# Hybrid RWKV-7 and neighbourhood-attention block: two affine forms of a tanh moved from VectorE to ScalarE, and the filler matmuls laid anew

## Chip, cores and metric

The kernel runs on one core of a Trainium2 chip. The metric is the device time of one execution in microseconds (us). A time is given as the median of several runs.

## What is computed

One trunk layer on 512 tokens of width 2048: a norm, one combined projection, two branches that read it (RWKV-7 time mixing in two directions, and 2-D neighbourhood attention), an output projection, a gated per-layer embedding and a final norm. Cut to what matters here:

```python
z = rms_norm(h, norm_mix_g) @ w_in
zs = centred_shift_mix(z[..., :SHIFT_W], mu_prev, mu_next)
# RWKV branch, 16 heads of 64, two directions
decay = exp(-DECAY_SCALE * sigmoid(w0 + tanh(wd) @ w2))
iclr = sigmoid(a0 + ad @ a2)
kk = (k * k_k) normalised per head
k_dir = k * (1.0 + (iclr - 1.0) * k_a)
# per token: S = S diag(w) + (S a) b^T + v k^T;  y = S r,  with a = -kk, b = kk * iclr
y = scan(forward) + scan(reverse);  group norm, bonus, SiLU gate
# attention branch: clamped 8 x 16 windows, softmax, SiLU gate
h = h + concat(y_a, y_b) @ w_out
h = h + (p @ w_ple_proj) * sigmoid(rms_norm(h) @ w_ple_gate)
return rms_norm(h)
```

## The kernel before

Every large product is made in three passes on TensorE (PE): a weight tile of 128x512 is copied on ScalarE (ACT) to a rounded half `wh` (L140), VectorE (DVE) makes the rest `wl` (L141), and `one_step` issues for each 128-row block three matmuls of 512 columns (L159, L161, L163). There are three raw buffers and six of `wh` and of `wl`.

The RWKV part runs in **eight rounds**, one for each pair of heads `ct`. In round `ct` the scan of pair `ct` (`chain`, eight steps of three parts: `cw` L592, `cu` L609, `cs` L619) goes on beside the preparation of pair `ct + 1` (`prepare`, `stage`, `normal`, `solve`). Each part of a scan step ends in a short DVE copy or sum that the next part's matmuls read: `wt` L596, `uv` L613, `uv` L625. A prologue prepares pair 0 with no scan beside it. After the rounds come eight pairs of attention heads (`natten`), the output projection and the gated embedding.

In `prepare` each of the two directions `d` makes, from the small products `lw` and `la`: two tanh on ACT (L418 into `t1`, L420 into `t3`), `1 + tanh` (L421) and a running sum (L424) on DVE, two exponentials on ACT (L425, L426), then on DVE the two affine forms of `t3` (L428 into `t4`, which takes a buffer named `tq`; L429 in place), a small copy of chunk ends (L431), and products (L434 to L445) that the `L458` matmuls read.

TensorE's order is written out by hand: `ORDER` lists the steps of a round (`c4b` is part b of scan step 4, `p`/`s` are parts of `prepare`, `v`/`m` of `stage`, `f` of `finish`, `n` of `normal`, `q`/`z` of `solve`), and the number behind a name says how many of the large projections' matmuls ("fillers") are issued ahead of that step. `EDGE_FILL` gives other numbers for single rounds (-1 is the prologue, 100 to 107 the attention). Fillers come from one stream of projections that later steps need; what has not been issued by then is issued at once.

The order on ACT, DVE, GpSimd (POOL) and the load queue is a scheduler's. `W_AHEAD` and `HOP` rank instructions ahead of what was written before them: `W_AHEAD` the weight loads, `wh` and `wl`; `HOP` the short DVE instructions of the scan. Every engine then works its own list strictly in order.

Of the kernel before, what the change touches and what calls it, by code (L numbers as in the profile page):

```python
# [10 lines left out]
AF = mybir.ActivationFunctionType  # L11
ALU = mybir.AluOpType
# [8 lines left out]
LAM = math.exp(-0.5)  # L21
EPS = 1e-6
LNX_EPS = 64e-5
W_AHEAD = 1275
FIRST = (24, 25, 8)
SUM_AT = (6, 35)
AT2 = (40, 24)
# [1 line left out]
KEEP_AT = 3  # L29
P_AHEAD = 200  # L30
ORDER = (
# [3 lines left out]
)  # L35
NAT_ORDER = (
    "np t0:11 t1:19 S0:16 S2:16 S1:3 T0:16 S3:25 T2:15 A0:26 T1:8 T3:24 A1:11"
)
FILL = {t.partition(":")[0]: int(t.partition(":")[2] or 0) for t in (ORDER + " " + NAT_ORDER).split()}
ORDER, NAT_ORDER = ([t.partition(":")[0] for t in o.split()] for o in (ORDER, NAT_ORDER))  # L40
EDGE_FILL = {
# [9 lines left out]
}  # L51
HOP = 118

VEC = {}
_o = 0
# [8 lines left out]
def block_kernel(ctx: ExitStack, tc: tile.TileContext, xT, pT, win, wout, wpg, wpp, vec, w2, rpb,  # L64
# [323 lines left out]
    def prepare(ct, k, r, kk, bon):  # L388
        w2r = sp.tile([128, 2, 2, 128], F32, name="w2r", tag="t3", bufs=1)
        S_.dma_start(w2r[0:64], w2[ct])  # L390
        S_.dma_start(w2r[64:128], w2[ct])
        w2s = sp.tile([128, 16, C], F32R, name="w2s", tag="ga", bufs=1).rearrange("p u i -> p (u i)")
        w2h = w2s[:, 0:512].rearrange("p (d i o) -> p d i o", d=2, i=2)
        w2l = w2s[:, 512:768].rearrange("p (i o) -> p i o", i=2)
        A.activation(w2h, w2r, AF.Copy)
        for d in range(2):
            rows = slice(64 * d, 64 * d + 64)
            G_.tensor_tensor(w2l[rows], w2r[rows, d], w2h[rows, d].bitcast(F32), ALU.subtract)

        kx = sp.tile([128, 2, NCH, 3, C], F32, name="kx", tag="kx", bufs=2)  # L400
        rx = kx[:, :, :, 1, :]
        pc = sp.tile([128, 2, NCH], F32, name="pc", tag="pc", bufs=2)
        m1s = []
        for d in range(2):
            yield
            rows = slice(64 * d, 64 * d + 64)
            lps = []
            for i in range(2):
                ps = aux()
                P.matmul(ps, w2h[:, d, i, :], lora[:, i, d, :], start=True, stop=False)  # L410
                P.matmul(ps, w2l[rows, i, :], lora[rows, i, d, :], start=False, stop=True)
                lps.append(ps)
            lw, la = lps
            t12 = sp.tile([128, 2, NCH, C + 1], F32, name="t12", tag="t12", bufs=1)
            t1, t2 = t12[:, 0], t12[:, 1]
            G_.memset(t1[:, :, 0:1], 0.0)
            wb = 26 + 8 * d + ct
            A.activation(t1[:, :, 1:], dirv(lw, d), AF.Tanh, scale=0.5, bias=vd[:, wb:wb + 1])  # L418
            t3 = b2("t3", 1)
            A.activation(chv(t3), dirv(la, d), AF.Tanh, scale=0.5, bias=vd[:, wb + 16:wb + 17])  # L420
            V.tensor_scalar(t1[:, :, 1:], t1[:, :, 1:], 1.0, None, ALU.add)  # L421
            t1f = t1.rearrange("p c i -> p (c i)")
            t2f = t2.rearrange("p c i -> p (c i)")
            V.tensor_tensor_scan(t2f, multf, t1f, 0.0, ALU.mult, ALU.add)  # L424
            A.activation(t1f, t2f, AF.Exp, scale=-0.5 * LAM)  # L425
            A.activation(t2[:, :, 1:], t2[:, :, 1:], AF.Exp, scale=0.5 * LAM)  # L426
            t4 = b2("tq", 2)
            V.tensor_scalar(t4, t3, vd[:, 58 + ct:59 + ct], vd[:, 66 + ct:67 + ct], ALU.mult, ALU.add)  # L428
            V.tensor_scalar(t3, t3, -0.5, -0.5, ALU.mult, ALU.add)  # L429
            ei = t2[:, :, 1:]  # L430
            V.tensor_copy(pc[:, d, :], t1[:, :, C])  # L431
            for h in range(2):
                hr = slice(64 * h, 64 * h + 64)
                (G_ if h else V).tensor_tensor(kx[hr, d, :, 2 * h, :], dirv(kk, d)[hr], t1[hr, :, 0:64], ALU.mult)  # L434
            V.tensor_tensor(chv(t4), chv(t4), ei, ALU.mult)
            V.tensor_tensor(chv(t3), chv(t3), ei, ALU.mult)
            V.tensor_tensor(rx[:, d, :, ::(-1 if d else 1)], dirv(r, d), t1[:, :, 1:], ALU.mult)
            m1 = sp.tile([128, NCH, 128], F32, name="m1", tag="m1", bufs=2)
            for h in range(2):
                hr = slice(64 * h, 64 * h + 64)  # L440
                bcol = slice(64 * h, 64 * h + 64)
                kcol = slice(64 - 64 * h, 128 - 64 * h)
                if d:
                    kcol = slice(127 - 64 * h, 63 if h == 0 else None, -1)
                V.tensor_tensor(m1[hr, :, bcol], chv(t3)[hr], dirv(kk, d)[hr], ALU.mult)  # L445
                G_.tensor_tensor(m1[hr, :, kcol], chv(t4)[hr], dirv(k, d)[hr], ALU.mult)  # L446
            m1s.append(m1)

        ga = sp.tile([128, 16, C], F32, name="ga", tag="ga", bufs=1)
        gr = sp.tile([128, 2, 2, NCH, C], F32, name="gr", tag="gr", bufs=2)  # L450
        for d in range(2):
            for c0 in range(0, NCH, 4):
                yield
                pair = [aux(), aux()]
                for c in range(4):
                    for h in range(2):
                        hr = slice(64 * h, 64 * h + 64)
                        P.matmul(pair[h][:, c * 128:(c + 1) * 128], m1s[d][hr, c0 + c, :],  # L458
                                 kx[hr, d, c0 + c, h:h + 2, :].rearrange("p s i -> p (s i)"), start=True, stop=True)
                cs = slice(c0, c0 + 4)  # L460
                for h in range(2):
                    hr = slice(64 * h, 64 * h + 64)
                    kr = slice(64 - 64 * h, 128 - 64 * h)
                    sv = pair[h].rearrange("p (c s i) -> p c s i", c=4, s=2)
                    V.tensor_tensor(ga[hr, d * NCH + c0:d * NCH + c0 + 4, :], sv[hr, :, h, :],
                                    mask[hr, None, 0:64].to_broadcast([64, 4, C]), ALU.mult)
                    V.tensor_tensor(gr[:, h, d, cs, :], sv[:, :, 1 - h, :],
                                    (mg1[h] if d else mask[:, 64:128])[:, None, :].to_broadcast([128, 4, C]), ALU.mult)
                    V.tensor_tensor(kx[kr, d, cs, 2 * h, :], sv[kr, :, h, :],  # L469
                                    (mk1 if d else mask[:, 0:64])[kr, None, :].to_broadcast([64, 4, C]), ALU.mult)  # L470
        td = sp.tile([128, 32, 32], F32, name="td", tag="td", bufs=1)
        V.transpose(out=td, in_=ga.rearrange("p u (ib i) -> p i ib u", ib=2))
        tmp = b2("t3", 1)

        def blocks(i0, ni, j0, nj, step=(32, 1)):
            return bass.AP(tensor=td.tensor, offset=td.offset + i0 * 32 + j0,
                           ap=[list(td.ap[0]), [16 * 33, 2], [step[0], ni], [step[1], nj]])

        for m in range(1, 15):
            ni = 15 - m  # L480
            tv = tmp[:, 0:2 * ni * m].rearrange("p (b i j) -> p b i j", b=2, j=m)
            V.tensor_tensor(tv, blocks(m + 1, ni, m, m, (32, 0)), blocks(m, ni, 0, m, (0, 1)), ALU.mult)  # L482
            V.tensor_tensor(blocks(m + 1, ni, 0, m), blocks(m + 1, ni, 0, m), tv, ALU.add)
        V.memset(td.rearrange("p i j -> p (i j)")[:, ::33], 1.0)
        return m1s, kx, rx, pc, bon, td, ga, gr
# [620 lines left out]
```

## Time and profile before

| | us |
|---|---|
| median of 3 runs | 1684.52 |
| lowest, highest | 1677.0, 1687.58 |
| the profiled execution: time, span | 1671.64, 1669.9 |

In the page's busy times PE stands at 1560.0 us (93% of the span), DVE at 1044.3 (63%), ACT at 685.2 (41%), POOL at 302.9 (18%). The granted TensorE clock is 0.957 on average. The profiled execution is one of its own and 12.9 us under the median, so terms are worked out on its time and then set against the median. Busy shares are means over stages: the rounds lie at 159.8 to about 882 us, the attention up to about 1291 us.

### The profile page before, as it was taken

Reading aid. Unit: us, or ns where it says so; the run is one execution under the profiler, and the core shown is the slowest. Engines: PE = TensorE matmul, PEld = TensorE weight load, DVE = VectorE, ACT = ScalarE, POOL = GpSimd, SP = SyncE. Lnnn points to the kernel's source line nnn. Section 1 sums busy time; section 2 is a strip of 40 time slices with the busy share of each in tenths; the row PEclk is TensorE's granted clock in tenths of the full one; section 3 lists DMA queues with packets and bytes.
Section 4 is the critical chain, followed back from the end, with each engine's and each line's share of the span. In section 5 each row is a group of like instructions: output and inputs, shape, how many; then the busy total and the mean of one; then the engine's idle time right before and its main releaser. Section 6 shows DMA issues by size and latency. Waiting matters only on the chain.

```text
span 1669.9 us, 30779 instructions
## 1 busy us (share of the span) xinstructions
PE 1560.0 (93%) x12392; PEld 1210.9 (73%) x12392; DVE 1044.3 (63%) x2071; ACT 685.2 (41%) x1231; POOL 302.9 (18%) x318
## 2 busy tenths in 40 slices
PE   7969898998989899898999999999999999999995
PEld 5757576766757576675767777777877888888885
DVE  8786886858688685878646444554456544454435
ACT  6624162442616244251426344443445333343331
POOL 2021414223141322314113011111110000100001
PEclk9979998999999898899999999999999999999998
DMA  6202020110202011020115332323222433532203
GB/s 210 94 29 67 21 83 27 62 48 26 84 20 83 27 58 52 21 82 27 59 40 173 100 95 89 88 76 95 81 78 80 136 122 118 165 119 89 88 32 101
DMA packets 74351, 131.32 MB, mean 79 GB/s; under 512 B 7904, under 2 KB 16352, under 8 KB 74208
## 3 DMA queue, kind: packets, MB, share of 16 engines
q1 hardware_dynamic: 74208, 129.36, 24.2%
q8 instruction: 97, 1.59, 0.4%
q14 instruction: 46, 0.38, 0.1%
HBM read 123.03 MB, written 6.29 MB: 77 GB/s over the span
## 4 chain that ended last, share of the span: by engine, by line
PE 74%; DVE 15%; issue 4%; ACT 4%; POOL 2%; DMA 1%; SPq 0%; DVEq 0%; ACTq 0%; POOLq 0%
PE mm L163 19%; PE mm L159 18%; PE mm L161 18%; DVE wl L141 2%; PE cs L619 2%; PE aux L458 1%; PE cw L592 1%; PE ns L792 1%; ACT wh L140 1%; DVE m L445 1%; POOL m L446 1%; PE no L818 1%; PE cu L609 1%; PE nt L808 1%; DVE t L482 1%
## 5 line engine op out<-in xcount | busy, mean ns | idle before, releaser
L141 DVE TENSOR_TENSOR wl<-wraw,wh 128x512 fp32r<-128x512 f32 x384 | 283.1, 738 | 305.5 <-ACT wh L140 255.2
L140 ACT ACTIVATE wh<-wraw 128x512 fp32r<-128x512 f32 x384 | 240.9, 628 | 506.3 <-PE mm L161 421.5
L159 PE MATMUL mm<-xh,wh 128*128 128x512 f32 x1024 | 420.7, 411 | 0.0
L163 PE MATMUL mm<-xh,wl 128*128 128x512 f32 x1024 | 419.9, 410 | 0.0
L161 PE MATMUL mm<-xl,wh 128*128 128x512 f32 x1024 | 418.4, 409 | 0.0
L159 PEld LDWEIGHTS mm<-xh,wh 128*128 128x128 f32 x1024 | 197.0, 192 | 42.6 <-issue 1.3
L163 PEld LDWEIGHTS mm<-xh,wl 128*128 128x128 f32 x1024 | 196.6, 192 | 42.8 <-issue 1.3
L161 PEld LDWEIGHTS mm<-xl,wh 128*128 128x128 f32 x1024 | 196.6, 192 | 42.7 <-issue 1.1
L159 PE MATMUL mm<-ch,wh 128*128 128x512 f32 x256 | 99.9, 390 | 0.0
L161 PE MATMUL mm<-cl,wh 128*128 128x512 f32 x256 | 99.9, 390 | 0.0
L163 PE MATMUL mm<-ch,wl 128*128 128x512 f32 x256 | 99.9, 390 | 0.0
L163 PE MATMUL mm<-hh,wl 128*128 128x512 f32 x224 | 87.3, 390 | 0.0
L161 PE MATMUL mm<-hl,wh 128*128 128x512 f32 x224 | 87.2, 389 | 0.0
L159 PE MATMUL mm<-hh,wh 128*128 128x512 f32 x224 | 87.1, 389 | 0.0
L604 POOL TENSOR_TENSOR stp<-uv,pc 64x128 f32<-64x128 f32 x96 | 56.1, 584 | 141.3 <-DVE uv L627 69.6
L768 POOL TENSOR_TENSOR bm<-text,nm 128x256 f32<-128x256 f32 x48 | 37.9, 818 | 237.5 <-DVE mx L794 193.0
L458 PE MATMUL aux<-kx,m 64*128 64x128 f32 x512 | 47.1, 306 | 14.7 <-DVE kx L469 7.5
L458 PEld LDWEIGHTS aux<-kx,m 64*128 64x128 f32 x512 | 38.6, 204 | 29.3 <-issue 20.1
L592 PE MATMUL cw<-uv,kx 128*64 128x64 f32 (+1 forms) x512 | 40.8, 248 | 18.9 <-DVE uv L625 17.7
L592 PEld LDWEIGHTS cw<-uv,kx 128*64 128x64 f32 (+1 forms) x512 | 28.4, 145 | 38.0 <-DVE uv L625 25.5
L163 PEld LDWEIGHTS mm<-ch,wl 128*128 128x128 f32 x256 | 48.1, 188 | 10.1
L159 PEld LDWEIGHTS mm<-ch,wh 128*128 128x128 f32 x256 | 48.1, 188 | 10.1 <-issue 0.2
(267 smaller groups left out, 2569.1 us busy)
## 6 DMA issues: line engine op xcount, KB each, us to landing
wraw<-in_win_dram SPq DMA_DIRECT2D x264, 256.0 KB
wraw<-in_wout_dram SPq DMA_DIRECT2D x64, 256.0 KB
wraw<-in_wpg_dram SPq DMA_DIRECT2D x56, 256.0 KB
xr<-in_xT_dram SPq DMA_DIRECT2D x32, 256.0 KB
out_dram<-h SPq DMA_DIRECT2D x16, 256.0 KB
text<-in_rpb_dram SPq DMA_DIRECT2D x16, 252.0 KB
w2r<-in_w_dram SPq DMA_DIRECT2D x16, 128.0 KB
cat<-bon SPq DMA_DIRECT2D x8, 256.0 KB
```

Of the source, the lines that this page charges most:

```text
L140: A.activation(wh, src, AF.Copy)
L141: V.tensor_tensor(wl, src, wh.bitcast(F32), ALU.subtract)
L159: P.matmul(ps, wh[:, sl], xh[kt], start=(kt == 0), stop=False)
L161: P.matmul(ps, wh[:, sl], xl[kt], start=False, stop=False)
L163: P.matmul(ps, wl[:, sl], xh[kt], start=False, stop=(kt == nk - 1))
L445: V.tensor_tensor(m1[hr, :, bcol], chv(t3)[hr], dirv(kk, d)[hr], ALU.mult)
L446: G_.tensor_tensor(m1[hr, :, kcol], chv(t4)[hr], dirv(k, d)[hr], ALU.mult)
L458: P.matmul(pair[h][:, c * 128:(c + 1) * 128], m1s[d][hr, c0 + c, :], kx[hr, d, c0 + c, h:h + 2, :].rearrange("p s i -> p (s i)"), start=Tr ...
L592: P.matmul(wps[hr, d * 64:(d + 1) * 64], kx[rows, d, c, 2 * h, :], uv[rows, c, h, d, :], start=True, stop=True)
L604: G_.tensor_tensor(sps[hr], uv[hr, c, h, :, :], pc[hr, :, c:c + 1].to_broadcast([64, 2, C]), ALU.mult)
L619: P.matmul(nps[hr, d * 64:(d + 1) * 64], mt[:, d, c, hr], uv[:, c, h, d, :], start=True, stop=True)
L768: G_.tensor_tensor(bm[:, kd].rearrange("p g r c -> p r g c"), text[:, ::-1, e1:(e1 - 32 if e1 > 31 else None):-1].rearrange("p r (g c) -> ...
```

## The change

The two DVE instructions L428 and L429 become ACT instructions in the same place of the program: an Identity with a scale and a bias per partition, and a Copy with two constants. `W_AHEAD` goes from 1275 to 4117 and `HOP` from 118 to 168. The numbers of fillers ahead of the steps are changed, most of them by one to five, and the attention's steps stand in another order. The changed file has three lines more, so its line numbers from the table on are higher by 3.

```diff
-W_AHEAD = 1275
+W_AHEAD = 4117
...
-    "pa p1:4 c0a c0b:2 c0c:2 c1a:2 c1b:1 c1c:4 p2:1 c2a c2b:4 c2c c3a:1 c3b:1 s0:2 c3c:3 c4a:1 c4b c4c "
+    "pa p1:4 c0a c0b:3 c0c:2 c1a:2 c1b:1 c1c:4 p2:1 c2a c2b:4 c2c c3a:1 c3b:1 s0:2 c3c:3 c4a:1 c4b c4c:1 "
...
-HOP = 118
+HOP = 168
...
-            V.tensor_scalar(t4, t3, vd[:, 58 + ct:59 + ct], vd[:, 66 + ct:67 + ct], ALU.mult, ALU.add)
-            V.tensor_scalar(t3, t3, -0.5, -0.5, ALU.mult, ALU.add)
+            A.activation(t4, t3, AF.Identity, scale=vd[:, 58 + ct:59 + ct], bias=vd[:, 66 + ct:67 + ct])
+            A.activation(t3, t3, AF.Copy, scale=-0.5, bias=-0.5)
```

The rest of the diff is the table: in a round `c7a` goes from 0 fillers to 3, `v1` from 1 to 4, `v2` from 6 to 7, `m0` from 14 to 9, `m2` from 4 to 1, `na` from 3 to 0. In the prologue `p2` goes from 7 to 2. In the last round's scan the fillers go from 64 to 74.

On DVE, round 3 (its fourth), from the `wt` copy of scan step 3 to that of step 4. Before (`t_4810` is t1 and t2 of direction 1, `t_4813` its t3):

```order
L596 COPY wt<-cw 128x128
L421 TENSOR_SCALAR t_4810<-t_4810 128x8x64
L424 SCALAR_TENSOR_TENSOR t_4810<-mult,t_4810 128x520
L613 COPY uv<-cu 64x128 x2
L428 TENSOR_SCALAR tq<-t_4813,vd 128x512
L431 COPY pc<-t_4810 128x8
L429 TENSOR_SCALAR t_4813<-t_4813 128x512
L434 TENSOR_TENSOR kx<-kk,t_4810 64x8x64
L141 TENSOR_TENSOR wl<-wraw,wh 128x512
L435 TENSOR_TENSOR tq<-tq,t_4810 128x512
L625 TENSOR_TENSOR uv<-cs,stp 64x128 x2
```

The same place in the changed kernel (lines higher by 3):

```order
L599 COPY wt<-cw 128x128
L424 TENSOR_SCALAR t_4811<-t_4811 128x8x64
L427 SCALAR_TENSOR_TENSOR t_4811<-mult,t_4811 128x520
L616 COPY uv<-cu 64x128 x2
L345 SCALAR_TENSOR_TENSOR zraw<-mm,rstdb 128x512
L144 TENSOR_TENSOR wl<-wraw,wh 128x512
L434 COPY pc<-t_4811 128x8
L437 TENSOR_TENSOR kx<-kk,t_4811 64x8x64
L438 TENSOR_TENSOR tq<-tq,t_4811 128x512
L628 TENSOR_TENSOR uv<-cs,stp 64x128 x2
```

The two affine forms are gone from between the two copies of the scan, and the evacuation of the gate's projection (L342 before, L345 now) has come in there from a place behind scan step 5.

On ACT, the same round, from its first tanh. Before:

```order
L418 ACTIVATE t_4704<-aux,vd 128x8x64
L420 ACTIVATE t_4707<-aux,vd 128x512
L425 ACTIVATE t_4704<-t_4704 128x520
L426 ACTIVATE t_4704<-t_4704 128x8x64
L140 ACTIVATE wh<-wraw 128x512
L418 ACTIVATE t_4810<-aux,vd 128x8x64
L420 ACTIVATE t_4813<-aux,vd 128x512
L140 ACTIVATE wh<-wraw 128x512
L425 ACTIVATE t_4810<-t_4810 128x520
L426 ACTIVATE t_4810<-t_4810 128x8x64
```

The same place in the changed kernel:

```order
L421 ACTIVATE t_4704<-aux,vd 128x8x64
L423 ACTIVATE t_4707<-aux,vd 128x512
L431 ACTIVATE tq<-t_4707,vd 128x512
L432 ACTIVATE t_4707<-t_4707 128x512
L428 ACTIVATE t_4704<-t_4704 128x520
L143 ACTIVATE wh<-wraw 128x512
L429 ACTIVATE t_4704<-t_4704 128x8x64
L421 ACTIVATE t_4811<-aux,vd 128x8x64
L423 ACTIVATE t_4814<-aux,vd 128x512
L431 ACTIVATE tq<-t_4814,vd 128x512
L143 ACTIVATE wh<-wraw 128x512
L428 ACTIVATE t_4811<-t_4811 128x520
```

The forms stand right behind the second tanh and ahead of the first exponential, in direction 0 both of them; a weight copy (L143 now) stands ahead of the second exponential of direction 0, where it stood behind it. No load of an activation table is added anywhere.

## Rows read from the trace of the kernel before

**Rows 1.** Windows by stage; stretch, length, PE, PEld, DVE, ACT, POOL, clock, DMA, GB/s.

```profile
0.00:159.80 159.80, 132.56 (x985) 103.07 (x985) 126.48 (x217) 83.04 (x137) 32.84 (x31) 0.91 0.32 103
159.80:837.60 677.80, 614.41 (x7309) 453.73 (x7308) 512.97 (x1056) 260.82 (x450) 183.02 (x198) 0.92 0.15 49
456.10:555.10 99.00, 90.72 (x1053) 66.92 (x1052) 75.25 (x153) 39.02 (x67) 26.64 (x29) 0.91 0.15 49
837.60:1640.00 802.40, 801.57 (x4018) 643.23 (x4016) 385.76 (x757) 335.48 (x634) 80.55 (x85) 1.00 0.31 97
```

**Rows 2.** Waits of PE; us in total, times, longest.

```profile
PE cs L619 <- DVE uv L613: 18.2, 22, 1.6
PE cw L592 <- DVE uv L625: 17.7, 10, 2.8
...
PE aux L458 <- DVE m L445: 6.1, 1, 6.1
```

**Rows 3.** Timeline of PE, round 3, scan steps 1 to 5; idle time in brackets.

```profile
461.45 0.45 PE L609 MATMUL cu<-wt,xt 64*64 64x64 f32 x8 [0.20 <-DVE wt L596]
...
478.77 0.77 PE L592 MATMUL cw<-uv,kx 128*64 128x64 f32 x8 [2.24 <-DVE uv L625]
...
480.67 0.69 PE L609 MATMUL cu<-wt,xt 64*64 64x64 f32 x8 [0.75 <-DVE wt L596]
482.59 1.07 PE L619 MATMUL cs<-uv,mt 128*64 128x64 f32 x7 [1.23 <-DVE uv L613]
...
488.38 0.40 PE L161 MATMUL mm<-xl,wh 128*128 128x512 f32 x1
488.62 0.39 PE L163 MATMUL mm<-xh,wl 128*128 128x512 f32 x1
```

**Rows 4.** Timeline of DVE, the same stretch.

```profile
474.66 0.55 DVE L428 TENSOR_SCALAR tq<-t,vd 128x512 f32<-128x512 f32 x1
475.13 1.14 DVE L431 COPY pc<-t 128x8 f32<-128x8 f32 x1
476.19 0.41 DVE L429 TENSOR_SCALAR t<-t 128x512 f32<-128x512 f32 x1
476.52 0.68 DVE L434 TENSOR_TENSOR kx<-kk,t 64x512 f32<-64x512 f32 x1
...
478.44 0.61 DVE L625 TENSOR_TENSOR uv<-cs,stp 64x128 f32<-64x128 f32 x2
...
489.32 0.67 DVE L342 SCALAR_TENSOR_TENSOR zraw<-mm,rstdb 128x512 f32<-128x512 f32 x1
```

**Rows 5.** Timelines of ACT and of POOL, the same stretch.

```profile
461.11 0.64 ACT L425 ACTIVATE t<-t 128x520 f32<-128x520 f32 x1 [4.15 <-DVE t L424]
...
473.55 0.63 ACT L140 ACTIVATE wh<-wraw 128x512 fp32r<-128x512 f32 x1 [1.00 <-PE mm L161]
474.16 0.64 ACT L425 ACTIVATE t<-t 128x520 f32<-128x520 f32 x1
...
474.88 1.37 POOL L434 TENSOR_TENSOR kx<-kk,t 64x512 f32<-64x512 f32 x1 [2.38 <-ACT t L425]
```

**Rows 6.** Groups by line and form; busy us, mean ns, idle before.

```profile
L428 DVE TENSOR_SCALAR tq<-t,vd 128x512 f32<-128x512 f32 x16 | 8.7, 544 | 0.2
L429 DVE TENSOR_SCALAR t<-t 128x512 f32<-128x512 f32 x16 | 8.0, 502 | 0.3
...
L426 ACT ACTIVATE t<-t 128x512 f32<-128x512 f32 x16 | 10.1, 631 | 0.5
...
L298 ACT ACTIVATE r<-zraw,vd 128x512 f32<-128x512 f32 x8 | 5.8, 725 | 6.1 <-DVE zraw L297 6.1
```

**Rows 7.** Windows of 3.4 us around scan step 4; columns as in rows 1.

```profile
476.80:480.20 3.40, 1.15 (x16) 0.81 (x16) 3.31 (x6) 0.00 (x0) 1.64 (x2) 1.00 0.23 77
480.20:483.60 3.40, 1.69 (x20) 1.32 (x22) 2.85 (x6) 0.00 (x0) 2.35 (x3) 0.50 0.00 0
483.60:487.00 3.40, 3.40 (x36) 2.65 (x32) 2.95 (x10) 0.00 (x0) 1.12 (x2) 0.50 0.00 0
```

**Rows 8.** Waits of ACT; us in total, times, longest.

```profile
ACT wh L140 <- PE mm L161: 453.2, 178, 15.3
```

More of the change, by code (lines that the diff above doesn't have):

```diff
@@ L31 @@
 ORDER = (
[3 rows of a table removed]
[3 rows of a table added]
 )
 NAT_ORDER = (
-    "np t0:11 t1:19 S0:16 S2:16 S1:3 T0:16 S3:25 T2:15 A0:26 T1:8 T3:24 A1:11"
+    "np:10 t0:21 t1:19 S0 S1:8 S2:22 T0:10 S3:20 T2:12 A0:14 T3:22 T1:12 A1:19"
 )
```

25 rows, old and new, of tables (EDGE_FILL, ORDER) are left out of this document.

## Prediction

> **What bounds the kernel now.** I read the windows by stage first [rows 1]. From 837.6 us to 1640 us, half of the span, PE is busy for 801.57 of 802.40 us at full clock: attention, output projection and gate are bound by TensorE, and since the change leaves every matmul in place, moving fillers there cannot win or lose much. The room is ahead of that. In the seven rounds with a preparation beside the scan (159.8 to 837.6 us) PE is idle for 677.80 - 614.41 = 63.4 us, about 9 us a round, and the clock is 0.92. In the prologue and the start it is idle for 159.80 - 132.56 = 27.2 us. Next come PE's waits [rows 2]: the largest name DVE's short scan instructions (uv after `cu`, uv after `cs`), and one of 6.1 us is the prologue's wait for the products of L445. So DVE's list is what PE waits for, though DVE is busy for only 75.25 of a round's 99.0 us: the waits gather where the preparation's long DVE instructions stand between the scan's short ones. In round 3 these are the waits ahead of step 4 and inside it, 2.24 + 0.75 + 1.23 = 4.2 us out of the round's 8.3 [rows 1, 3]. These repeat from round to round; over the whole kernel the first kind comes to 17.7 us [rows 2].
>
> **The change, part by part. What leaves DVE:** 16 times L428 and 16 times L429, 8.7 + 8.0 = 16.7 us or 2.1 us a round [rows 6]. That is the most a straight return could give in eight preparations. I follow one round to see how much of it PE gets.
>
> Direction 0: the forms stand at scan step 1. PE waits there for 0.20 us only [rows 3], since it is busy with its own list; the time that DVE wins up to step 2 is spent waiting for PE's next `cw`. The extra filler at `c0b` is paid there and saved where it came from. I take 0; the bounds are 0 and 1.0 us.
>
> Direction 1: here PE waits for the L625 that starts at 478.44. From the start of L428 at 474.66 to there DVE is busy without a break for 3.78 us [rows 4]. Start to start, L428 holds 475.13 - 474.66 = 0.47 and L429 0.33 us, so 0.8 us leave. But the gate's L342, 0.67 us, comes in at this very place. L431, a copy of 8 columns, takes 1.14 us here while POOL runs its own L434 from 474.88 for 1.37 us; it now stands later, so most of POOL's time lies beside L342 and the `wl` ahead of it, and I count 0.6 us less for it. Sum 0.8 - 0.7 + 0.6 = 0.7 us a round. If L431 keeps its length the sum is 0.1; if it shrinks to a few tenths and L342's place costs nothing, it is 1.6. I take 0.7, since POOL's instruction moves with the running sum and the overlap will not vanish whole.
>
> Then step 4: the new filler at `c4c` stands in the wait of 1.23 us, and takes work from a place where PE is never idle. A filler is worth 488.62 - 488.38 = 0.24 us at full clock and twice that at half [rows 3], so 0.35 us a round. L342 is gone from behind step 5 (489.32, rows 4); DVE waits for PE's L458 products more than the other way there, so I take 0.2 us, bounds 0 and 0.7. The three fillers at `c7a` and the fewer at `m0` and `m2` are moved between places where PE has next to no idle time: 0. A round gives 0.7 + 0.35 + 0.2 = 1.25 us, seven rounds 8.8 us.
>
> **What ACT takes on.** The Identity has two operands per partition. An ACT form with one takes 725 ns and one with none 631 ns [rows 6], so I estimate 0.82 us for two, and 0.63 us for the Copy. The pair costs 1.45 us, 23 us over 16 pairs. ACT is busy for 39 of 99 us in a round. In direction 0 it sits idle for 4.15 us ahead of L425, waiting for the running sum, and both forms fit in there [rows 5]. In direction 1 the Identity fits ahead of the weight copy that waits 1.00 us for PE, but the Copy stands between the two exponentials and delays L426 by 0.6 us; L435 reads that, and DVE reaches it only behind L434, later than L426's new end. So 0, and 0.3 us a round against if that cover is gone.
>
> **Prologue.** Here nothing but DVE is late. Each direction loses 0.54 + 0.50 us of forms, but the first exponential (0.64 us, rows 5) ran beside them and must now be waited for, so 0.4 us is left; in direction 0 the mix of `v` now fills that gap, and 1.1 us is left. Together 1.5 us, bounds 0 and 3.
>
> **The clock.** In the 3.4 us ahead of step 4 PE is busy for 1.15 us, and right behind it the granted clock falls to 0.50, that is from 2.4 to 1.2 GHz, and stays there for two such stretches, 6.8 us [rows 7]. With 0.7 us less idle time the fall may stay out in some rounds. The eight small matmuls of a `cu` take 0.45 us at full clock and 0.69 at half (461.45 and 480.67, rows 3), 0.24 us more, and about five such parts lie in the 6.8 us: 1.2 us a round. I take it in two to three of seven rounds, 3 us; bounds 0 and 8.4. It can also go the other way: a fall that comes earlier or lasts one window longer costs as much.
>
> **Attention and the rest.** PE has no idle time to win; a wait made anew by the other order of scores would show as idle PE. I take 0, and 4 us against.
>
> **Sum.** 8.8 + 1.5 + 3 = 13.3 us off the profiled execution's 1671.64, so 1658.3 us. The median of the runs is 12.9 us above that execution, and the forecast is set against it: 1684.5 - 13.3 = **1671.2 us**, 0.8% under. About 1% is what a measurement of this kernel can tell from no change.
>
> **Rivals.** *Full return.* DVE's whole 2.1 us a round come back, because each scan step hangs on DVE's list from step 1 to step 7, and the clock no longer falls: 7 x (2.1 + 0.35 + 1.2) + 3 = 28.5 us, 1656 us. For it speaks that DVE is all but unbroken from 458 to 490 us; against it, that PE's wait at step 1 is only 0.20 us, and that L342 moved in.
>
> *No return.* The change takes the load off DVE, but PE's written order ends the round: the wait for L625 only becomes the wait for the next L613, or L342 waits there for the gate's last filler. 2 us are left from the filler at `c4c`, 1682 us. It speaks for this that the three waits are only 4.2 of a round's 99 us, and that PE's own list fills 90.72 of these.
>
> *Slower: ACT's list is blocked.* In direction 0 a weight copy now stands ahead of L426. It may start only when PE has left the buffer that it writes; ACT waited so 178 times for 453.2 us, 2.5 us at a time [rows 8]. If L426 is late by more than DVE needs for the two instructions ahead of L435 (some 1.3 us), L435, L436, L437 and all scan copies behind them are late by the rest. At 2.5 us a round, with no gain left, seven rounds cost 17.5 us: 1702 us. Against it: in round 3 the filler that frees the buffer is issued just before that point.
>
> *Slower by the wrong engine.* If ACT rather than DVE ended the stretch, the forms' longer duration would be paid in full: 23 - 16.7 = 6.5 us, 1691 us. ACT's idle 4.15 us speak against it. The Trainium skill, "ScalarE: Activation LUTs", section "Rules for kernel authors", advises such adds and multiplies for VectorE and not ScalarE, for its speed per element; the trace agrees on the durations (544 ns on DVE against 725 on ACT for a like form, rows 6), but shows DVE as the late engine.
>
> **Chances.** Forecast 0.45, full return 0.25, no return 0.17, blocked ACT 0.09, wrong engine 0.04. The forecast's own range, with its bounds, is 1660 to 1680. The range that leaves out 2 in 10 reaches from beyond the full return, 1653, to a little above no change, 1689. Faster by over 1% (under 1667.7): the full return, and a third of the forecast, 0.40. Slower by over 1% (over 1701.4): most of the blocked case and a small tail, 0.12. Within 1%: 0.48.
>
> **What the changed profile would show.** DVE busy down by 16.7 us, ACT's up by 23. In round 3 the wait of 2.24 us ahead of step 4's `cw` should be about 1.5 us, the 1.23 us ahead of `cs` under 1. A `pc` copy that still takes over 1 us, or an L342 that waits for PE, moves the result to "no return". A half-clock stretch behind step 4 in fewer than seven rounds is the clock's term. ACT waits for PE in front of the second exponential, with DVE's L435 waiting for it, would be the blocked list. The forecast is wrong at once if PE is idle in the attention.

## Result, and the profile after

| | median us (runs) | ratio to before, 95% |
|---|---|---|
| before, same chip | 1685.56 (20) | 1 |
| changed kernel | 1675.17 (20) | 0.9928 [0.9911, 0.9945] |
| forecast | 1671.2 | 0.992 |

The change is worth 0.7% by the ratio, some 12 us, and 10.4 us, or 0.6%, by the two medians; the interval of the ratio (0.55 to 0.89%) holds both, and the forecast's 0.8%. The profiled execution of the changed kernel is not a good one: it took 1680.22 us (span 1678.4), 5 us over its median, where that of before was 12.9 us under its own. So the two spans can't be subtracted; the stages have to be read for what makes the difference. First the page's busy times (engine, us, share, instructions) and its row of the granted clock:

```profile
PE 1577.7 (94%) x12392; PEld 1221.0 (73%) x12392; DVE 1025.3 (61%) x2039; ACT 705.1 (42%) x1263; POOL 302.5 (18%) x318
...
PEclk9977898998889889888999999999999999999997
```

DVE lost 19.0 us and ACT gained 19.9 (forecast 16.7 and 23). Now the windows by stage, which answer to [rows 1] (start and prologue, the seven rounds, round 3, what follows):

```profile
0.00:166.20 166.20, 138.83 (x989) 107.09 (x989) 123.37 (x213) 87.63 (x144) 33.47 (x31) 0.88 0.31 101
166.20:844.80 678.60, 625.57 (x7303) 459.78 (x7302) 500.37 (x1028) 277.73 (x476) 180.74 (x198) 0.91 0.15 48
463.30:562.30 99.00, 92.33 (x1053) 68.02 (x1052) 73.09 (x149) 41.67 (x71) 26.55 (x29) 0.90 0.15 49
844.80:1649.00 804.20, 802.28 (x4026) 643.72 (x4022) 382.47 (x757) 334.31 (x634) 81.83 (x85) 1.00 0.30 97
```

In the rounds PE is idle for 678.60 - 625.57 = 53.0 us, where it was 63.4: 10.4 us less. Yet the rounds are no shorter (678.6 against 677.8), because PE is *busy* for 11.2 us more with the same matmuls. That is the clock. Counted from the stretches that the profile shows at 0.50, the rounds spent 102 us at half clock before and 127 us here. Taken as lost work is half of the half-clock time: 614.4 - 51 = 563 us before, 625.6 - 63 = 562 us here. That is an estimate, since PE also waits in such stretches (1.69 of 3.40 us busy in one of them, [rows 7]). So a stage's length is read as three parts, **work at full clock + half of the time at half clock + idle**, and only the third is what the change aimed at. The prologue is idle as before (27.4 against 27.2 us); that it is 6.4 us longer in this execution goes with a lower granted clock there, 0.88 against 0.91. What follows the rounds has 1.9 us of idle PE against 0.8.

PE's waits (us in total, times, longest), beside [rows 2]:

```profile
PE cs L622 <- DVE uv L616: 13.1, 20, 1.1
PE cw L595 <- DVE uv L628: 12.4, 15, 1.6
...
PE aux L461 <- DVE m L448: 6.1, 1, 6.1
...
PE aux L522 <- ACT mt L523: 3.6, 7, 0.5
```

The two waits for the scan's short DVE instructions fell from 18.2 to 13.1 and from 17.7 to 12.4 us. The prologue's wait of 6.1 us stands unchanged. The last line is new: 0.5 us a round for a copy of the solve on ACT, where `m2` lost three of its four fillers.

Round 3 on PE, scan steps 2 to 4, beside [rows 3] (idle time in brackets):

```profile
476.26 0.71 PE L622 MATMUL cs<-uv,mt 128*64 128x64 f32 x7 [0.99 <-DVE uv L616]
...
485.32 0.77 PE L595 MATMUL cw<-uv,kx 128*64 128x64 f32 x8 [1.60 <-DVE uv L628]
...
487.33 0.69 PE L612 MATMUL cu<-wt,xt 64*64 64x64 f32 x8 [0.86 <-DVE wt L599]
487.95 0.79 PE L164 MATMUL mm<-xl,wh 128*128 128x512 f32 x1
489.26 1.07 PE L622 MATMUL cs<-uv,mt 128*64 128x64 f32 x7 [0.51 <-DVE uv L616]
```

The wait ahead of step 4 is 1.60 us (2.24 before, about 1.5 forecast); the one ahead of `cs` is 0.51 (1.23 before, under 1 forecast), with the new filler, L164, ahead of it. DVE in the same round, beside [rows 4]:

```profile
473.43 0.29 DVE L599 COPY wt<-cw 128x128 f32<-128x128 f32 x1 [0.51 <-PE cw L595]
...
481.84 0.69 DVE L345 SCALAR_TENSOR_TENSOR zraw<-mm,rstdb 128x512 f32<-128x512 f32 x1
482.44 1.35 DVE L144 TENSOR_TENSOR wl<-wraw,wh 128x512 fp32r<-128x512 f32 x1
483.71 0.16 DVE L434 COPY pc<-t 128x8 f32<-128x8 f32 x1
483.79 0.68 DVE L437 TENSOR_TENSOR kx<-kk,t 64x512 f32<-64x512 f32 x1
484.39 0.68 DVE L438 TENSOR_TENSOR tq<-tq,t 128x512 f32<-128x512 f32 x1
484.99 0.60 DVE L628 TENSOR_TENSOR uv<-cs,stp 64x128 f32<-64x128 f32 x2
```

DVE is still unbroken up to the L628 that PE waits for. L345 does not wait for PE here. The small `pc` copy is down from 1.14 to 0.16 us, but `wl`, which now stands beside POOL's product (482.05, 1.19 us), takes 1.35 us where it took 0.68. ACT, beside [rows 5]:

```profile
464.17 0.82 ACT L431 ACTIVATE tq<-t,vd 128x512 f32<-128x512 f32 x1
465.02 0.63 ACT L432 ACTIVATE t<-t 128x512 f32<-128x512 f32 x1
468.51 0.64 ACT L428 ACTIVATE t<-t 128x520 f32<-128x520 f32 x1 [2.86 <-DVE t L427]
...
479.75 0.82 ACT L431 ACTIVATE tq<-t,vd 128x512 f32<-128x512 f32 x1
480.49 0.63 ACT L143 ACTIVATE wh<-wraw 128x512 fp32r<-128x512 f32 x1
481.34 0.64 ACT L428 ACTIVATE t<-t 128x520 f32<-128x520 f32 x1 [0.22 <-DVE t L427]
481.88 0.62 ACT L432 ACTIVATE t<-t 128x512 f32<-128x512 f32 x1
```

The Identity takes 0.82 us and the Copy 0.62 to 0.63, as estimated. With both taken on, ACT still waits for DVE, 2.86 us in direction 0 and 0.22 us in direction 1. But one wait of DVE for ACT is new (us in total, times, longest), the small copy `pc` for the first exponential:

```profile
DVE pc L434 <- ACT t L428: 3.0, 7, 0.7
```

### The profile page after: what moved, and what is told of

It is laid out like the page before. It is cut to its first block, busy times and chain, and to the rows that moved or that the text cites. A ratio compares the mean times of both kernels' runs of the same rounds, so it can differ in the third digit from the quotient of the medians.

```text
span 1678.4 us, 30803 instructions
## 1 busy us (share of the span) xinstructions
PE 1577.7 (94%) x12392; PEld 1221.0 (73%) x12392; DVE 1025.3 (61%) x2039; ACT 705.1 (42%) x1263; POOL 302.5 (18%) x318
## 4 chain that ended last, share of the span: by engine, by line
PE 82%; DVE 10%; issue 3%; ACT 2%; DMA 1%; POOL 1%; SPq 0%; DVEq 0%; ACTq 0%
PE mm L166 21%; PE mm L162 20%; PE mm L164 20%; PE aux L461 2%; PE cs L622 2%; PE cw L595 1%; PE ns L795 1%; DVE m L448 1%; DVE wl L144 1%; PE no L821 1%; PE cu L612 1%; PE aux L522 1%; PE ns L794 1%; PE nt L811 1%; PE aux L566 1%
## 5 line engine op out<-in xcount | busy, mean ns | idle before, releaser
L143 ACT ACTIVATE wh<-wraw 128x512 fp32r<-128x512 f32 x384 | 240.9, 628 | 516.0 <-PE mm L164 439.9
L162 PE MATMUL mm<-xh,wh 128*128 128x512 f32 x1024 | 426.2, 416 | 0.0
L166 PE MATMUL mm<-xh,wl 128*128 128x512 f32 x1024 | 426.1, 416 | 0.0
L164 PE MATMUL mm<-xl,wh 128*128 128x512 f32 x1024 | 423.9, 414 | 0.0
L164 PEld LDWEIGHTS mm<-xl,wh 128*128 128x128 f32 x1024 | 199.8, 195 | 43.9 <-issue 1.9
L164 PE MATMUL mm<-cl,wh 128*128 128x512 f32 x256 | 100.0, 391 | 0.0
L164 PE MATMUL mm<-hl,wh 128*128 128x512 f32 x224 | 87.1, 389 | 0.0
L771 POOL TENSOR_TENSOR bm<-text,nm 128x256 f32<-128x256 f32 x48 | 41.4, 889 | 210.4 <-DVE mx L797 207.9
L162 PEld LDWEIGHTS mm<-ch,wh 128*128 128x128 f32 x256 | 48.1, 188 | 10.2 <-issue 0.2
L164 PEld LDWEIGHTS mm<-cl,wh 128*128 128x128 f32 x256 | 48.1, 188 | 10.2 <-issue 0.2
L449 POOL TENSOR_TENSOR m<-tq,k 64x512 f32<-64x512 f32 x32 | 50.1, 1567 | 18.0 <-DVE tq L438 16.3
```

Source lines behind the costliest of these rows:

```text
L143: A.activation(wh, src, AF.Copy)
L162: P.matmul(ps, wh[:, sl], xh[kt], start=(kt == 0), stop=False)
L164: P.matmul(ps, wh[:, sl], xl[kt], start=False, stop=False)
L166: P.matmul(ps, wl[:, sl], xh[kt], start=False, stop=(kt == nk - 1))
L771: G_.tensor_tensor(bm[:, kd].rearrange("p g r c -> p r g c"), text[:, ::-1, e1:(e1 - 32 if e1 > 31 else None):-1].rearrange("p r (g c) -> ...
```

## Experiments

My theory: DVE's list is the late one, and the move gives back part of it, some 9 us in the rounds; the filler tables add little. The rivals: the tables or the two ranks do it and the move nothing; the clock does it; ACT is the engine that ends the stretch. Each experiment was timed in five rounds beside the kernel before, not all on one chip, so the ratios compare rather than the medians. Two readings go with every ratio: the us at half clock (twice what the mean granted clock of a run lacks, times its span, mean over the runs), and the parts of the seven rounds in the one profiled execution. Within one kernel, a run with one us more at half clock took 0.24 to 0.46 us longer, by a straight line through its runs (0.35 for the changed kernel, 0.31 for the kernel before); not 0.5, most likely because PE also waits in these stretches.

| kernel | median us (runs) | ratio, 95% | half clock, runs | rounds: idle, half clock, length |
|---|---|---|---|---|
| before | 1686.9 (57) | 1 | 183 | 63.4, 102, 677.8 |
| changed | 1675.2 (20) | 0.9928 [0.9911, 0.9945] | 166 | 53.0, 127, 678.6 |
| move_only | 1683.7 (12) | 0.9983 [0.9958, 1.0009] | 188 | 55.4, 147, 689.7 |
| tables_only | 1679.2 (12) | 0.9956 [0.9925, 0.9987] | 159 | 54.8, 126, 683.9 |
| consts_only | 1687.3 (12) | 0.9988 [0.9962, 1.0015] | 181 | 62.9, 109, 680.6 |
| nat_before | 1671.3 (6) | 0.9914 [0.9881, 0.9947] | 162 | 57.2, 109, 674.8 |
| order_before | 1675.3 (6) | 0.9917 [0.9898, 0.9937] | 169 | 51.5, 120, 675.7 |
| c4c_out | 1673.9 (6) | 0.9912 [0.9889, 0.9935] | 159 | 58.7, 123, 677.3 |
| m2_back | 1670.8 (6) | 0.9916 [0.9891, 0.9941] | 155 | 54.5, 102, 670.6 |
| double_identity | 1679.7 (12) | 0.9946 [0.9921, 0.9972] | 182 | 52.0, 126, 675.8 |
| cover | 1717.5 (5) | 1.0206 [1.0182, 1.0229] | 189 | 85.2, 140, 720.2 |
| solve_fill | 1660.4 (4) | 0.984 [0.9809, 0.987] | 137 | 50.8, 99, 666.8 |
| solve_more | 1669.3 (5) | 0.9881 [0.9859, 0.9904] | 137 | 63.1, 96, 676.5 |
| solve_c4 | 1672.5 (6) | 0.9898 [0.9875, 0.9921] | 137 | 59.9, 99, 676.3 |

How far the idle time alone can be trusted is seen from nat_before: its rounds are the changed kernel's, instruction for instruction, up to the seventh's solve, and with 17 us less at half clock it shows 4.1 us more idle. Idle is compared at like half clock.

**The move alone, and the tables alone.** To the kernel before, only the two forms on ACT; and the changed kernel with the forms back on DVE.

```diff
-            V.tensor_scalar(t4, t3, vd[:, 58 + ct:59 + ct], vd[:, 66 + ct:67 + ct], ALU.mult, ALU.add)
-            V.tensor_scalar(t3, t3, -0.5, -0.5, ALU.mult, ALU.add)
+            A.activation(t4, t3, AF.Identity, scale=vd[:, 58 + ct:59 + ct], bias=vd[:, 66 + ct:67 + ct])
+            A.activation(t3, t3, AF.Copy, scale=-0.5, bias=-0.5)
```

> The kernel before with only the two affine forms on ScalarE; all tables as before. If the relief of VectorE's list alone carries the gain, this has most of it: ratio to before 0.993 to 0.996 (7 to 12 us less). If the new tables carry it, 0.999 to 1.003. A mixed case: the scheduler now puts the 1.4 us product L437 ahead of the scan's sum L625 in the place that the forms left, so PE's wait of 2.24 us ahead of scan step 4 stays at 1.5 to 2.5 us, and the ratio is 0.997 to 1.000.

> The changed kernel with the two affine forms back on VectorE; all new tables. If the relief of VectorE carries the gain: 0.998 to 1.002, with the wait ahead of step 4's cw at 2 us or more again. If the new tables carry it: 0.992 to 0.995, with the wait still near 1.6 us. The filler at c4c should keep the wait inside step 4 short (0.5 us instead of 1.2) in either case.

By time the move alone can't be told from nothing, 0.17% with an interval that reaches over 1. The stage says why. The rounds of move_only, in the windows, and PE ahead of its step 4:

```profile
164.50:854.20 689.70, 634.33 (x7308) 468.73 (x7307) 500.16 (x1028) 279.89 (x478) 185.75 (x198) 0.89 0.14 48
```

```profile
489.76 0.77 PE L592 MATMUL cw<-uv,kx 128*64 128x64 f32 x8 [1.25 <-DVE uv L625]
...
493.37 1.07 PE L619 MATMUL cs<-uv,mt 128*64 128x64 f32 x7 [1.23 <-DVE uv L613]
```

PE is idle for 55.4 us, 8.0 less than before, and the wait ahead of step 4 fell from 2.24 to 1.25 us: the move by itself shortens the wait that the forecast named first (the 1.23 us inside the step stay). But this execution has 147 us at half clock in the rounds against 102, and 45 x 0.5 = 22 us of longer matmuls hide the gain; over the runs the mean is 188 against 183 us. The tables alone have 159 us at half clock and are 0.4% faster. The rounds of tables_only, PE ahead of its step 4 in round 3, and a window of its round 4:

```profile
161.30:845.20 683.90, 629.12 (x7302) 460.67 (x7301) 511.26 (x1056) 259.42 (x449) 181.13 (x198) 0.91 0.14 48
```

```profile
481.38 0.96 PE L595 MATMUL cw<-uv,kx 128*64 128x64 f32 x8 [2.11 <-DVE uv L628]
```

```profile
570.50:577.30 6.80, 6.80 (x44) 4.50 (x46) 6.26 (x12) 2.47 (x4) 1.89 (x3) 0.50 0.11 40
```

In round 3 the wait is still 2.11 us. In five of the seven rounds, round 4 among them, the clock falls ahead of step 4 and not behind it; PE is then busy with slower matmuls up to the step, and no wait over 0.6 us for L628 is left there. So idle PE comes to 54.8 us with the forms still on DVE, 8.6 less than before: half clock fills waits, and the idle time of the rounds does not tell the move from the tables.

What does tell them apart is the wait where PE comes to step 4 at full clock, as in round 3 of all four kernels: the move takes 1.0 us of it with the old tables (2.24 to 1.25) and 0.5 us with the new ones (2.11 to 1.60). In time the move is worth 0.17% or 2.9 us with the old tables, at 5 us more half clock, and 0.28% or 4.7 us with the new ones, at 7 us more. At 0.31 to 0.35 us for each us of half clock that makes some 4.5 us and some 7 us at equal half clock. These are estimates, good to some 4 us: the interval of move_only reaches over 1, and those of tables_only and the changed kernel overlap. So neither part alone explains the 0.7%: the move shortens a wait, and something in the tables lowers the time at half clock.

**Which part of the tables.** The two ranks alone put into the kernel before; the attention's order and numbers of before in the changed kernel; the rounds' `ORDER` of before in the changed kernel.

```diff
-W_AHEAD = 1275
+W_AHEAD = 4117
-HOP = 118
+HOP = 168
```

> The kernel before with W_AHEAD 4117 and HOP 168 alone; the forms stay on VectorE and all filler numbers stay. If the two ranks carry part of the tables' gain of 0.4%: 0.996 to 0.998, with less time at half clock than before (180 us on average). If the fillers carry it: 0.999 to 1.002.

```diff
-    "np:10 t0:21 t1:19 S0 S1:8 S2:22 T0:10 S3:20 T2:12 A0:14 T3:22 T1:12 A1:19"
+    "np t0:11 t1:19 S0:16 S2:16 S1:3 T0:16 S3:25 T2:15 A0:26 T1:8 T3:24 A1:11"
```

> The changed kernel with the attention's order and fillers as before the change. PE is never idle in the attention in either, so by the forecast's reasoning this costs and gains nothing: 0.992 to 0.994. If the new attention order carries part of the gain: 0.995 to 0.998.

```diff
-    "pa p1:4 c0a c0b:3 c0c:2 ... c4a:1 c4b c4c:1 "
-    "... c7a:3 s3:3 c7b c7c:4 fa v0:5 v1:4 f0:6 v2:7 m0:9 m1 f1:12 m2:1 "
-    "m3:1 na n0:30 n1:1 q0:2 q1:5 q:5 z:10"
+    "pa p1:4 c0a c0b:2 c0c:2 ... c4a:1 c4b c4c "
+    "... c7a s3:3 c7b c7c:4 fa v0:5 v1:1 f0:6 v2:6 m0:14 m1 f1:12 m2:4 "
+    "m3:1 na:3 n0:30 n1:1 q0:2 q1:5 q:5 z:10"
```

> The changed kernel with the rounds' filler numbers of before (the ORDER table); the exceptions for the prologue, the last round and the attention stay new. If the rounds' fillers carry the fewer us at half clock (188 us with the old tables, 166 with the new): 180 to 190 us at half clock and 0.997 to 0.999, as with the move alone. If the prologue's and the last round's fillers carry it: 160 to 170 us and 0.992 to 0.994.

The ranks alone give nothing (0.9988), the attention's order nothing (0.9914 without it, 0.9928 with it), and the rounds' own numbers nothing (0.9917 without them). What order_before still has, and move_only has not, are the `EDGE_FILL` numbers of the prologue and of rounds 0, 6 and 7, the ranks together with the forms on ACT, and the attention's order, which was just ruled out. Between these two kernels lie 0.66% and 19 us at half clock. Whether the edges or the ranks carry this was not tried, and stays open.

**Single fillers.** Without the filler at `c4c` (given to `m0`); and with `m2` as before.

```diff
-    "... c4a:1 c4b c4c:1 " "... m0:9 m1 f1:12 m2:1 "
+    "... c4a:1 c4b c4c "   "... m0:10 m1 f1:12 m2:1 "
```

> The changed kernel without the filler at c4c, and with 10 at m0 instead of 9. VectorE's order around step 4 stays word for word. By the forecast the filler stands in a wait of 1.23 us and is worth 0.35 us a round: the wait ahead of step 4's cs goes from 0.5 back to about 1.2 us, and the time is 2 to 3 us more: 0.994 to 0.995. If the filler only delays what it fills, the time is that of the changed kernel or 1 to 2 us less: 0.991 to 0.993.

```diff
-    "... m0:9 m1 f1:12 m2:1 "
+    "... m0:6 m1 f1:12 m2:4 "
```

> The changed kernel with 4 fillers at m2 (as before the change) and 6 at m0. The changed kernel's trace has a wait of 0.51 us in each of seven rounds, for ScalarE's copy of the mt tile, that was not there before. If the three fillers that left m2 opened it, it goes and the time is 2 to 4 us under the changed kernel: ratio to before 0.989 to 0.992. If ScalarE is late there for its own reasons, the wait stays or moves and the ratio is that of the changed kernel, 0.993.

PE of c4c_out, round 3, step 4:

```profile
485.38 1.06 PE L622 MATMUL cs<-uv,mt 128*64 128x64 f32 x7 [1.24 <-DVE uv L616]
```

The wait is 1.24 us without the filler and 0.51 with it, so the filler does fill it; but the time is the same (0.9912 against 0.9928). The place lies at half clock, so the 0.73 us less of wait are mostly the filler's own longer time; where it came from, at full clock, it took 0.24 us [rows 3]. With `m2` back at four fillers the new wait at L522 is gone, another of 0.5 us stands in its stead (L137 for POOL's `sl`, 2.9 us in total), and again the ratio can't be told from the changed kernel's. Both are worth less than these runs resolve.

**Is ACT near its end?** The Identity issued twice; the output is the same.

```diff
             A.activation(t4, t3, AF.Identity, scale=vd[:, 58 + ct:59 + ct], bias=vd[:, 66 + ct:67 + ct])
+            A.activation(t4, t3, AF.Identity, scale=vd[:, 58 + ct:59 + ct], bias=vd[:, 66 + ct:67 + ct])
```

> The changed kernel with the Identity made twice, into the same tile, so ScalarE works 16 x 0.82 = 13 us more at the disputed place. If ScalarE has room there (it waited 2.86 us for the running sum in direction 0 and 0.22 us in direction 1): 0 to 3 us more than the changed kernel, 0.993 to 0.995. If ScalarE ends the stretch, each costs its 0.82 us: 7 to 13 us more, 0.997 to 1.001.

Its ACT and PE around step 4 of round 3 (lines higher by one from the second Identity, L432, on):

```profile
474.98 0.64 ACT L428 ACTIVATE t<-t 128x520 f32<-128x520 f32 x1 [0.23 <-DVE t L427]
475.52 0.80 ACT L432 ACTIVATE tq<-t,vd 128x512 f32<-128x512 f32 x1
```

```profile
478.97 0.77 PE L596 MATMUL cw<-uv,kx 128*64 128x64 f32 x8 [1.61 <-DVE uv L629]
```

With 0.8 us more on ACT in each direction, ACT still waits for DVE and PE's wait is 1.61 us, as in the changed kernel (1.60); idle PE in the rounds is 52.0 us against 53.0. So ACT does not end the stretch. The scheduler put the Copy behind the second exponential here, so the exponentials come no later: what is shown is that ACT has room for 13 us more, not that it has room at every place. The ratio is 0.9946, higher than the changed kernel's with intervals that overlap, beside 16 us more at half clock.

**Filling the wait instead.** Eight more fillers into step 4, taken from `n0`.

```diff
-    "... c4a:1 c4b c4c:1 " "m3:1 na n0:30 n1:1 q0:2 q1:5 q:5 z:10"
+    "... c4a:6 c4b:3 c4c:1 " "m3:1 na n0:22 n1:1 q0:2 q1:5 q:5 z:10"
```

> The changed kernel with 6 fillers instead of 1 ahead of step 4's cw and 3 instead of 0 ahead of its cu, taken from n0. If PE's waits there (1.6 and 0.86 us a round) are free room, eight fillers of 0.24 us cover 1.9 us a round, 10 to 13 us in all, and the half-clock stretch behind step 4 goes: ratio 0.980 to 0.987. If VectorE's list, laid anew by the scheduler with two products and a weight rest ahead of step 4's uv copies, ends the step, the scan is late by as much as the fillers take: 0.992 to 1.000.

It lost 2%. The fillers did cover the wait ahead of `cw` (5.1 us in total, none over 0.5, where the changed kernel has 12.4 and 1.6). PE's other waits name the place that the fillers left:

```profile
PE aux L137 <- POOL sl L369: 23.5, 12, 4.0
PE cs L622 <- DVE uv L616: 17.0, 21, 1.4
...
PE cu L612 <- DVE wt L599: 12.6, 14, 2.5
```

L137 waits 23.5 us for POOL's `sl`, which the fillers at `n0` had covered, and the scan's waits grew as well (17.0 and 12.6 us against 13.1 and 6.3).

**The solve's clock.** In the changed kernel's round 3 the clock falls a second time, in the solve. Three windows of 3.4 us there:

```profile
541.90:545.30 3.40, 3.40 (x138) 2.74 (x137) 2.53 (x5) 2.55 (x5) 0.00 (x0) 1.00 0.24 82
545.30:548.70 3.40, 2.39 (x155) 1.88 (x155) 1.88 (x3) 0.04 (x1) 0.00 (x0) 1.00 0.24 77
548.70:552.10 3.40, 3.40 (x75) 2.42 (x67) 1.28 (x3) 2.09 (x5) 0.00 (x0) 0.51 0.02 5
```

In the middle one PE runs 155 mostly tiny matmuls (32x16) and waits 1.01 us for DVE; then it is at half clock for 10.2 us. So I moved fillers from `z` to the steps among the small matmuls, on top of m2_back; then still more of them; then, on top of the first of these, two more into each of two parts of step 4.

```diff
-    "... m0:9 m1 f1:12 m2:1 " "m3:1 na n0:30 n1:1 q0:2 q1:5 q:5 z:10"
+    "... m0:6 m1 f1:12 m2:4 " "m3:1 na n0:30 n1:1 q0:2 q1:8 q:8 z:6"
```

> The version with 4 fillers at m2, and in the solve 8, 8 and 6 fillers at q1, q and z instead of 5, 5 and 10. The clock falls to half in most rounds in the solve, behind its small matmuls and PE's waits of 1.0 us and up to 2.2 us. If the added fillers fill these waits, the falls there (38 to 55 us in a profile) get fewer, at 0.3 to 0.4 us of time for each us at half clock, and the wait of 1.0 us goes: 5 to 15 us less, 0.983 to 0.989. If the waits are for the solve's own copies and the fillers only come on top, or the fewer at z open a wait there: 0.991 to 0.996.

```diff
-    "... q0:2 q1:8 q:8 z:6"
+    "... q0:2 q1:12 q:12 z:6"
```

> As the version with 8, 8 and 6 fillers at q1, q and z (0.984), with 12, 12 and 6. If more matmuls of 512 columns among the solve's small ones keep the clock up further: 110 to 130 us at half clock, 0.976 to 0.982. If the solve's waits are full by then and the added fillers delay the copies that it hangs on, or leave other waits uncovered: 0.985 to 0.995.

```diff
-    "... c4a:1 c4b c4c:1 "
+    "... c4a:3 c4b:2 c4c:1 "
```

> As the version with 8, 8 and 6 fillers in the solve (0.984), with 3 fillers at c4a instead of 1 and 2 at c4b instead of 0; VectorE's order up to step 5 stays but for one weight rest. There PE waits 1.15 us ahead of step 4's cu. If that is free room and part of what lets the clock fall behind it: 3 to 8 us less, 0.979 to 0.982. If the scan is late by what the fillers take: 0.984 to 0.988.

The same place in round 3 of solve_fill, in windows and on PE:

```profile
535.60:539.00 3.40, 3.28 (x138) 2.53 (x130) 3.14 (x5) 1.32 (x3) 0.00 (x0) 1.00 0.35 122
539.00:542.40 3.40, 3.19 (x196) 2.94 (x197) 1.30 (x3) 1.51 (x4) 0.00 (x0) 1.00 0.02 6
542.40:545.90 3.50, 2.91 (x72) 2.18 (x71) 0.49 (x2) 1.10 (x4) 0.12 (x1) 1.00 0.25 80
```

```profile
539.21 0.20 PE L553 MATMUL aux<-es,xt 32*32 32x16 f32 x1 [0.33 <-DVE bon L381]
```

The wait is 0.33 us, PE is busy for 2.9 us and more in each window, and the clock stays at 1.00. But one round proves little. In nat_before, whose list is the changed kernel's in this place, a wait of 1.02 us stands in the first of these two windows of round 3, and the clock stays up as well:

```profile
538.10:541.60 3.50, 2.48 (x121) 1.86 (x112) 2.99 (x5) 1.09 (x2) 0.00 (x0) 1.00 0.25 87
541.60:545.00 3.40, 3.33 (x198) 2.70 (x186) 0.95 (x2) 1.48 (x4) 0.00 (x0) 1.00 0.02 5
```

And in one profile each of m2_back and solve_fill the clock falls in the solve of five rounds of seven, for 38 and 31 us. What speaks for the fillers is the runs: 137 us at half clock against 155 in m2_back, from which solve_fill differs in these three numbers alone, and 0.984 against 0.9916. The 18 us are worth some 6 us by the line through the runs, and the medians differ by 10. It is the fastest of the three kernels, though its interval touches that of solve_more. The other two, solve_more and solve_c4, have as little half clock, and lose it again to waits: 63.1 and 59.9 us of idle PE in the rounds against 50.8. Half clock and idle are two accounts, and a filler can move a loss from one to the other.

## Why the prediction was right, point by point

**What bounds.** DVE's list was what PE waited for at step 4: with the forms off it the wait of round 3 fell from 2.24 to 1.25 us on the old tables and from 2.11 to 1.60 on the new ones, and another Identity on ACT left the idle PE of the rounds as it was (52.0 us).

**The rounds: 8.8 us forecast.** Idle PE fell by 10.4 us in the profiled executions, but that does not prove the term: the move alone takes 8.0 us of it and the tables alone 8.6, at different half clock, and about 5.1 us (seven times 0.73) are the filler at `c4c`, which c4c_out gives back without losing time. What bears the forecast out is the place: 0.7 us a round was forecast ahead of step 4, and the move took 1.0 and 0.5 us there. In time the move is worth some 4 to 7 us by the estimate above; the forecast has 6.3 us for it, once the 7 x 0.35 us of the filler are left out. The filler was oversized: at half clock it takes longer itself, and no gain in time is measurable. The inner parts were right in direction: direction 0 gave DVE a wait for PE (0.51 us at 473.43); L345 came in and the `pc` copy shrank, by 1.0 us rather than 0.6, while 0.7 us went to `wl` beside POOL, which I had not counted.

**ACT: 0.** Right, durations included (0.82 and 0.63 us). ACT's list was not blocked: in round 3 the weight copies that stand among the exponentials wait for nothing, and L438, which needs the second exponential, never waits for ACT. That ACT is the late engine is refuted by the doubled Identity. Its room is small, though: DVE waits for the first exponential ahead of `pc`, 3.0 us in seven waits, and never did before. The Trainium skill's advice ("ScalarE: Activation LUTs", section "Rules for kernel authors") to keep such work on VectorE holds for the duration, 816 ns here against 544 on DVE [rows 6]; what decided was which engine is late.

**Prologue: 1.5 us.** Wrong: 0, by the one profile. The wait for L448 is 6.1 us as before, and the idle time to the first round 27.4 against 27.2.

**The clock: 3 us.** The size is of the right order, the mechanism failed. I said that the fall behind step 4 stays out in two or three rounds; it comes in all seven rounds of the changed profile. Yet the runs' mean at half clock fell from 183 to 166 us, worth 17 x 0.31 to 0.35 = 5 to 6 us. It is as low in most kernels with the new edges and ranks (155 to 169 us), but not in the doubled Identity (182) or in cover (189). What lowers it is not shown.

**Sum.** Some 4 to 7 us from the move and 5 to 6 of clock, 9 to 13 us, beside 9.3 to 15.0 measured (the interval on 1685.56). That the forecast of 13.3 lies there is in part luck: the 1.5 us of the prologue and the 2.5 of the filler did not come, and the clock gave 2 to 3 us more than forecast, in another way. The new wait of 0.5 us a round at L522 was not foreseen.

**Not settled.** A reckoning at equal half clock is good to some 4 us at best: by it the doubled Identity would be some 2 to 3 us *faster* than the changed kernel. One more Identity on ACT went with 16 us more at half clock while the idle PE of the rounds did not grow, so that time may hang on small shifts, and no single number of the table can be named as what lowers it.

## What to carry to other kernels

Split a stage's length into work at full clock, half of the time at half clock, and idle time before two executions are compared; a change that removes waits can look like nothing because the clock took it, and idle time can fall merely because half clock fills the waits. When an engine with half-empty busy time is the one waited for, moving work to a slower engine that waits for it can pay, at 820 ns for 544: here 0.5 to 1.0 us at the place where it was late, and some 4 to 7 us in all by estimate. Fillers paid here among the small matmuls of the solve (0.984 against 0.9916), and cost time where they left another wait bare (1.0206 in cover).

## What was not expected of the hardware

The clock can fall behind a stretch where PE is far from idle: 2.39 of 3.40 us busy with 155 matmuls in the solve, then 10.2 us at half clock. Nor does such a wait settle it: in nat_before PE was busy for 2.48 of 3.50 us in the same place, and the clock stayed up. Three more fillers at each of two steps there went with 137 us at half clock in place of 155, as a mean over the runs.

The runs of one kernel spread by some 14 us (1667.4 to 1681.7 for the changed one), and time at half clock accounts for most of it: a line through the 20 runs leaves 1.6 us.

A short instruction's duration can go with what stands beside it: `pc`, 8 columns wide, has a median of 172 ns now and 586 before, over 16 copies in each. In round 3 `pc` took 1.14 us beside POOL's product [rows 4, 5]; now `wl` stands beside it, and takes 1.35 us in place of 0.68.
